# Relu and row sum of 64 MB: the first 8 MB in two contiguous loads, and a piece of the tail moved from ScalarE to VectorE

## The chip, the cores and the metric

The kernel runs on one core of a Trainium2 chip. The metric is device time in microseconds of that core; lower is better. A run on one core has a span (first to last instruction in the profile) about 1.35 us shorter than its time. All runs with several rounds are of the fast state; single runs have no state ("unknown"). Nothing here uses TensorE, so its clock plays no part.

## The reference

```python
def setup_inputs():
    batch, seq, dim = 32, 512, 1024
    return {"x": np.random.randn(batch, seq, dim).astype(np.float32)}

def reference(x):
    relu_x = np.maximum(x, 0)
    return np.sum(relu_x, axis=-1).astype(np.float32)
```

67.1 MB are read, 65 KB written. There are 16384 rows of 4 KB, 128 for each partition.

## The kernel before

All loads go out on SyncE's queue. A buffer holds 16 rows a partition (8 MB); there are three. The first 8 MB are a region of their own, in which partition p owns rows 16p to 16p+15, so 64 KB lie together and the pitch from partition to partition is 64 KB too. The other 56 MB have a pitch of 448 KB.

```python
N1 = P * ROWS                                            # 128 x 16 rows
xf = x_flat[:N1].rearrange("(p m) d -> p m d", p=P)      # first 8 MB
xv = x_flat[N1:].rearrange("(p m) d -> p m d", p=P)      # the rest
# [...]
for j in range(NB):                                      # seven loads of 8 MB
    # [...]
    loaded = load(buf[:, :, :], rows(m, ROWS), j >= NBUF and freed[j - NBUF])
    # [...]
    for n in TWO[j]:                                     # [16], [8, 8] or [7, 7] rows
        clamp(buf[:, c : c + n, :], act_waits)           # ScalarE: relu in place
        total(buf[:, c : c + n, :], m + c, n)            # VectorE: sum of each row
        # [...]
    # [...] single rows of the last two of these loads
```

The last 8 MB come in loads of 8 and 4 rows, then the last four rows in four loads that grow smaller: two rows and the start of the third ("split") row; the end of the split row with the fourth row; and the middle of the split row in two pieces. Partial sums of the split row are written as extra columns behind the last piece, and one VectorE instruction sums that piece and the columns.

```python
act_row(buf[:, c, :], res[:, m : m + 1], loaded)                 # ScalarE: row 0
# [...]
act_row(flat[:, at + split : at + b], others[0], None)           # ScalarE: 340 columns of the split row
piece_act = n_act
dve_row(buf[:, c + 1, :], res[:, m + 1 : m + 2], loaded)         # VectorE: row 1
# [...]
loaded = load(flat[:, at + end : at + 4 * D], src[:, end:])
act_row(buf[:, c + 3, :], res[:, m + 3 : m + 4], loaded)         # ScalarE: row 3
dve_row(flat[:, at + end : at + 3 * D], others[1], loaded)       # VectorE: 240 columns
# [...] loads of the pieces, 220 and 224 columns; two stores
for i in range(len(PIECES) - 1):
    dve_row(parts[i][:, :], others[2 + i], arrived[i])           # VectorE: first piece
nc.vector.wait_ge(sems.act, piece_act)
nc.vector.wait_ge(sems.dve, n_dve)
nc.vector.tensor_scalar(out=last[:, :], ..., accum_out=res[:, NT - 2 : NT - 1]
    ).wait_op(arrived[-1], 16, "sem-ge").then_inc(sems.dve, 1)   # VectorE: last piece + partial sums
# [...]
store(NT - 2, 2, n_act, n_dve)
```

Of the kernel before, what the change touches and what calls it, by code (L numbers as in the profile page):

```python
# [7 lines left out]
P = 128  # L8

ROWS = 16  # L10
NBUF = 3


TWO = [[16], [16], [16], [8, 8], [8, 8], [7, 7], []]
ACT = [0, 0, 0, 0, 0, 2, 9]
DVE = [0, 0, 0, 0, 0, 0, 7]



TAIL = [8, 4]  # L20
ACT_PIECE, END_PIECE = 340, 240
PIECES = [220, 224]

EARLY = 1

# [1 line left out]
def kernel(tc: tile.TileContext, x: bass.AP, out: bass.AP):  # L27
    nc = tc.nc
    sems = Semaphores(tc)

    tc.close()
    tc.compile()
    nc.cur_bb = nc.bb_map[tc.start_bb_name]
    body = nc.cur_bb.bb.instructions
    ends = list(body)
    body.clear()
    n_stores = relu_sum(nc, sems, x, out)
    body.extend(ends)


    nc.cur_bb = nc.bb_map[tc.start_bb_name + "_end"]
    nc.cur_bb.bb.instructions.clear()
    nums = sorted(s.num for s in (*sems.loads, sems.act, sems.dve))
    cleared = range(nums[0], nums[-1] + 1)
    assert len(cleared) == len(nums)
    nc.sync.sem_clear(cleared)
    nc.sync.wait_ge(sems.stored, 16 * n_stores).then_inc(sems.stored, -16 * n_stores)
    open_without_barrier(tc, EARLY)


class Semaphores:
    def __init__(self, tc: tile.TileContext):
        n = len(TWO) + len(TAIL) + 2 + len(PIECES)
        self.loads = [tc.alloc_semaphore(f"load{i}") for i in range(n)]
        self.act = tc.alloc_semaphore("act")
        self.dve = tc.alloc_semaphore("dve")
        self.stored = tc.alloc_semaphore("stored")


def relu_sum(nc, sems: Semaphores, x: bass.AP, out: bass.AP):  # L60
    x_flat = x.flatten_outer_dims()
    N, D = x_flat.shape
    NT = N // P
    NB = len(TWO)
    assert N == P * NT == P * ROWS * (NB + 1)
    assert sum(TAIL) == ROWS - 4 and ACT_PIECE + END_PIECE + sum(PIECES) == D

    bufs = [nc.alloc_sbuf_tensor(f"io{i}", [P, ROWS, D], F32) for i in range(NBUF)]
    res = nc.alloc_sbuf_tensor("res", [P, NT], F32)

    extra = len(PIECES) + 1
    parts = [
        nc.alloc_sbuf_tensor(f"piece{i}", [P, w + extra * (i + 1 == len(PIECES))], F32)
        for i, w in enumerate(PIECES)
    ]


    N1 = P * ROWS
    xf = x_flat[:N1].rearrange("(p m) d -> p m d", p=P)
    xv = x_flat[N1:].rearrange("(p m) d -> p m d", p=P)  # L80
    o_flat = out.rearrange("b s -> (b s)")
    of = o_flat[:N1].rearrange("(p m) -> p m", p=P)
    ov = o_flat[N1:].rearrange("(p m) -> p m", p=P)

    def rows(m, n):
        if m < ROWS:
            return xf[:, m : m + n, :]
        return xv[:, m - ROWS : m - ROWS + n, :]

    def sums(m, n):  # L90
        if m < ROWS:
            return of[:, m : m + n], res[:, m : m + n]
        return ov[:, m - ROWS : m - ROWS + n], res[:, m : m + n]

    n_load = n_act = n_dve = n_store = 0

    def load(dst, src, after=None):
        nonlocal n_load
        dma = nc.sync.dma_start(out=dst, in_=src)  # L99
        if after:  # L100
            dma.wait_op(sems.dve, after[1], "sem-ge")
        dma.then_inc(sems.loads[n_load], 16)
        n_load += 1
        return sems.loads[n_load - 1]

    def store(m, n, act, dve):
        nonlocal n_store
        dst, src = sums(m, n)
        nc.sync.wait_ge(sems.act, act)
        nc.sync.dma_start(out=dst, in_=src).wait_op(sems.dve, dve, "sem-ge").then_inc(  # L110
            sems.stored, 16
        )
        n_store += 1

    def clamp(ap, loaded):
        nonlocal n_act
        i = nc.scalar.activation(out=ap, in_=ap, func=RELU)  # L117
        if loaded is not None:
            i.wait_op(loaded, 16, "sem-ge")
        i.then_inc(sems.act, 1)  # L120
        n_act += 1

    def total(ap, m, n):
        nonlocal n_dve
        nc.vector.tensor_reduce(  # L125
            out=res[:, m : m + n], in_=ap, axis=mybir.AxisListType.X, op=ADD
        ).wait_op(sems.act, n_act, "sem-ge").then_inc(sems.dve, 1)
        n_dve += 1

    def act_row(ap, accum_out, loaded):  # L130
        nonlocal n_act
        i = nc.scalar.activation(out=ap, in_=ap, func=RELU, accum_out=accum_out)  # L132
        if loaded is not None:
            i.wait_op(loaded, 16, "sem-ge")
        i.then_inc(sems.act, 1)
        n_act += 1

    def dve_row(ap, accum_out, loaded):
        nonlocal n_dve
        i = nc.vector.tensor_scalar(  # L140
            out=ap,
            in0=ap,
            scalar1=0.0,
            scalar2=None,
            op0=MAX,
            op1=ADD,
            accum_out=accum_out,
        )
        if loaded is not None:
            i.wait_op(loaded, 16, "sem-ge")  # L150
        i.then_inc(sems.dve, 1)
        n_dve += 1

    freed = []
    m = 0
    for j in range(NB):
        buf = bufs[j % NBUF]
        loaded = load(buf[:, :, :], rows(m, ROWS), j >= NBUF and freed[j - NBUF])
        c = 0
        act_waits = dve_waits = loaded  # L160
        for n in TWO[j]:
            clamp(buf[:, c : c + n, :], act_waits)
            total(buf[:, c : c + n, :], m + c, n)
            act_waits = None
            c += n
        for _ in range(ACT[j]):
            act_row(buf[:, c, :], res[:, m + c : m + c + 1], act_waits)
            act_waits = None
            c += 1
        for _ in range(DVE[j]):  # L170
            dve_row(buf[:, c, :], res[:, m + c : m + c + 1], dve_waits)
            dve_waits = None
            c += 1
        assert c == ROWS
        freed.append((n_act, n_dve))
        m += ROWS


    buf = bufs[NB % NBUF]
    c = 0  # L180
    for n in TAIL:
        loaded = load(
            buf[:, c : c + n, :], rows(m, n), None if c else freed[NB - NBUF]
        )
        for i in range(n):
            if i % 2 == 0 or (n == 8 and i == 7):
                act_row(buf[:, c, :], res[:, m : m + 1], loaded if i == 0 else None)
            else:
                dve_row(buf[:, c, :], res[:, m : m + 1], loaded if i == 1 else None)
            c += 1  # L190
            m += 1

    flat = buf[:, :, :].rearrange("p c d -> p (c d)")
    src = rows(m, 4).rearrange("p c d -> p (c d)")
    at = c * D
    split = 2 * D
    b = split + ACT_PIECE
    end = split + D - END_PIECE
    last, w = parts[-1], PIECES[-1]
    others = [last[:, w + i : w + i + 1] for i in range(extra)]  # L200
    loaded = load(flat[:, at : at + b], src[:, :b])
    act_row(buf[:, c, :], res[:, m : m + 1], loaded)
    sums_act = n_act
    act_row(flat[:, at + split : at + b], others[0], None)
    piece_act = n_act
    dve_row(buf[:, c + 1, :], res[:, m + 1 : m + 2], loaded)
    sums_dve = n_dve
    loaded = load(flat[:, at + end : at + 4 * D], src[:, end:])
    act_row(buf[:, c + 3, :], res[:, m + 3 : m + 4], loaded)
    dve_row(flat[:, at + end : at + 3 * D], others[1], loaded)  # L210
    arrived = []
    for part, n in zip(parts, PIECES):
        arrived.append(load(part[:, :n], src[:, b : b + n]))
        b += n
    assert b == end



    store(0, ROWS, *freed[0])
    store(ROWS, NT - ROWS - 2, sums_act, sums_dve)  # L220

    for i in range(len(PIECES) - 1):
        dve_row(parts[i][:, :], others[2 + i], arrived[i])
    nc.vector.wait_ge(sems.act, piece_act)
    nc.vector.wait_ge(sems.dve, n_dve)  # L225
    nc.vector.tensor_scalar(  # L226
        out=last[:, :],
        in0=last[:, :],
        scalar1=0.0,
        scalar2=None,  # L230
        op0=MAX,
        op1=ADD,
        accum_out=res[:, NT - 2 : NT - 1],
    ).wait_op(arrived[-1], 16, "sem-ge").then_inc(sems.dve, 1)
    n_dve += 1
    store(NT - 2, 2, n_act, n_dve)
    return n_store
# [49 lines left out]
```

## Time and profile before

| | before |
|---|---|
| time, median of the first 3 runs | 161.2 us (161.14 to 161.52) |
| span of the profiled run | 159.7 us |
| VectorE / ScalarE / DMA queue, share of the span | 73% / 66% / 98% |
| first 8 MB landed | 21.84 us |
| last load landed | 157.57 us |
| last load to end of span | 2.17 us |

The landings are read from the records of semaphore increments in the trace: a load has landed when the last of its 16 DMA engines has made its increment. The start of the ScalarE instruction that waits for it, some 0.02 us later, shows the same in the timeline. The end of the chain of waits, with columns start, length, what:

```profile
157.73 0.03 issue
157.76 0.05 DVEq L225
157.81 0.07 issue
157.88 0.40 DVE piece L226 x2
```

Between the accumulator's end at 157.73 us and the last sum stand a semaphore instruction of VectorE's queue and two bits of issue: 0.15 us in which VectorE computes nothing.

### The profile page before, as it was taken

To read this page: it belongs to the slowest core of one execution; us is meant where nothing else is said; L and a number is where in the kernel's file an instruction comes from. 1 tells how busy PE (TensorE), PEld (TensorE's weight loads), DVE (VectorE), ACT (ScalarE), POOL (GpSimd) and SP (SyncE) were. 2 spreads that over 40 slices of the span, in tenths; PEclk is the share of its full clock that TensorE was granted. 3 is DMA by queue.
4 is the path that set the end of the run, shared out by engine and by line. 5 is a ranking of instruction groups with operands and counts; after the bars stand their busy time and mean duration, and the time that the engine had idled before them with its cause. 6 is when DMAs were issued, how large, how long until landed. Compare 5 with 4: busy or idle time off the path is not lost.

```text
span 159.7 us, 120 instructions
## 1 busy us (share of the span) xinstructions
DVE 117.2 (73%) x41; ACT 104.7 (66%) x52; POOL 0.2 (0%) x4
## 2 busy tenths in 40 slices
DVE  0000000009999499994999999999999999999985
ACT  3000059990699708996099941999339992499996
POOL 0000000000000000000000000000000000000000
DMA  7996996996997999979979969969969969898993
GB/s 263 525 525 263 525 525 263 525 492 295 525 460 328 525 394 394 525 345 443 525 328 460 525 279 509 525 263 525 525 263 525 492 295 525 345 443 386 414 417 113
DMA packets 2304, 67.18 MB, mean 421 GB/s; under 512 B 640, under 2 KB 896, under 8 KB 1024
## 3 DMA queue, kind: packets, MB, share of 16 engines
q1 hardware_dynamic: 2304, 67.18, 98.0%
HBM read 67.11 MB, written 0.07 MB: 421 GB/s over the span
## 4 chain that ended last, share of the span: by engine, by line
DMA 44%; DVE 33%; ACT 17%; another core or an unknown queue 3%; SPq 1%; issue 0%; DVEq 0%
DMA io<-in_x_dram 44%; DVE res L125 32%; ACT io L117 17%; SPq L99 1%; DVE io L140 0%; DVE piece L226 0%; DVE piece L140 0%; DVEq L225 0%
## 5 line engine op out<-in xcount | busy, mean ns | idle before, releaser
L125 DVE TENSOR_REDUCE res<-io 128x8 f32<-128x8192 f32 (+2 forms) x9 | 101.1, 11287 | 40.0 <-ACT io L117 40.0
L117 ACT ACTIVATE io<-io 128x8192 f32<-128x8192 f32 (+2 forms) x9 | 81.7, 9110 | 47.7 <-DMA io<-in_x_dram 47.7
L132 ACT ACTIVATE io<-io 128x1024 f32<-128x1024 f32 (+1 forms) x21 | 21.3, 1017 | 5.7 <-DMA io<-in_x_dram 5.7
L140 DVE TENSOR_SCALAR_CACHE_REDUCE io<-io 128x1024 f32<-128x1024 f32 (+1 forms) x14 | 15.5, 1157 | 0.9 <-DMA io<-in_x_dram 0.9
L132 ACT ACTIVATION_READ_ACCUMULATOR io<-io 128x1 f32 x21 | 3.9, 187 | 0.0
L117 ACT ACT_TABLE_LOAD x1 | 1.3, 1283 | 0.1
L140 DVE DVE_READ_ACCUMULATOR io<-io 128x1 f32 x14 | 1.2, 82 | 0.0
L226 DVE TENSOR_SCALAR_CACHE_REDUCE piece<-piece 128x227 f32<-128x227 f32 x1 | 0.4, 390 | 0.2 <-DVE piece L140 0.2
L140 DVE TENSOR_SCALAR_CACHE_REDUCE piece<-piece 128x220 f32<-128x220 f32 x1 | 0.4, 378 | 0.0
L271 POOL MEMSET const-bfloat16-1.0<- 128x1 bf16 x1 | 0.1, 102 | 0.0
L271 POOL MEMSET const-uint8-127<- 128x1 uint8 x1 | 0.1, 102 | 0.0
L271 POOL MEMSET const-float32-0.0<- 128x1 f32 x1 | 0.1, 99 | 0.2 <-issue 0.2
L271 POOL MEMSET const-float32-1.0<- 128x1 f32 x1 | 0.1, 99 | 0.0
L140 DVE DVE_READ_ACCUMULATOR piece<-piece 128x1 f32 x1 | 0.1, 85 | 0.0
L226 DVE DVE_READ_ACCUMULATOR piece<-piece 128x1 f32 x1 | 0.1, 83 | 0.0
## 6 DMA issues: line engine op xcount, KB each, us to landing
io<-in_x_dram SPq DMA_DIRECT2D x1, 4096.0 KB, 21.6
io<-in_x_dram SPq DMA_DIRECT2D x1, 2048.0 KB, 26.1
io<-in_x_dram SPq DMA_DIRECT2D x1, 1194.0 KB, 28.5
io<-in_x_dram SPq DMA_DIRECT2D x1, 632.0 KB, 29.6
io<-in_x_dram SPq DMA_DIRECT2D x7, 26.9
piece<-in_x_dram SPq DMA_DIRECT2D x1, 112.0 KB, 29.2
piece<-in_x_dram SPq DMA_DIRECT2D x1, 110.0 KB, 29.4
out_dram<-res SPq DMA_DIRECT2D x1, 55.0 KB, 1.6
```

Source lines behind the costliest of these rows:

```text
L99: dma = nc.sync.dma_start(out=dst, in_=src)
L117: i = nc.scalar.activation(out=ap, in_=ap, func=RELU)
L125: nc.vector.tensor_reduce(out=res[:, m : m + n], in_=ap, axis=mybir.AxisListType.X, op=ADD).wait_op(sems.act, n_act, "sem-ge").then_inc(se ...
L132: i = nc.scalar.activation(out=ap, in_=ap, func=RELU, accum_out=accum_out)
L140: i = nc.vector.tensor_scalar(out=ap, in0=ap, scalar1=0.0, scalar2=None, op0=MAX, op1=ADD, accum_out=accum_out,)
L226: nc.vector.tensor_scalar(out=last[:, :], in0=last[:, :], scalar1=0.0, scalar2=None, op0=MAX, op1=ADD, accum_out=res[:, NT - 2 : NT - 1],) ...
L271: nc = _bacc.Bacc("TRN2", target_bir_lowering=False, num_devices=1)
```

## The change

Its intent: give the loads at the start a smaller pitch and earlier work, take from ScalarE a piece for which VectorE's last sum had to wait, and let that last instruction wait for VectorE's own accumulator in place of the load. The diff is shortened, and a call of several lines is put on one:

```diff
-TWO = [[16], [16], [16], [8, 8], [8, 8], [7, 7], []]
+HEAD = 8
+TWO = [[8, 8], [16], [16], [8, 8], [8, 8], [7, 7], []]
-ACT_PIECE, END_PIECE = 340, 240
-PIECES = [220, 224]
+START_PIECE, END_PIECE = 280, 260
+PIECES = [240, 244]
 ...
-    xf = x_flat[:N1].rearrange("(p m) d -> p m d", p=P)
+    xf = x_flat[:N1].rearrange("(s p m) d -> p s m d", p=P, m=HEAD)
-    of = o_flat[:N1].rearrange("(p m) -> p m", p=P)
+    of = o_flat[:N1].rearrange("(s p m) -> p s m", p=P, m=HEAD)
 ...
+        if j == 0:
+            heads = [load(buf[:, h : h + HEAD, :], rows(h, HEAD)) for h in range(0, ROWS, HEAD)]
 ...
+                act_waits = heads[i]
 ...
-    act_row(flat[:, at + split : at + b], others[0], None)
-    piece_act = n_act
     dve_row(buf[:, c + 1, :], res[:, m + 1 : m + 2], loaded)
     sums_dve = n_dve
+    dve_row(flat[:, at + split : at + b], others[0], None)
 ...
-    nc.vector.wait_ge(sems.act, piece_act)
-    nc.vector.wait_ge(sems.dve, n_dve)
+    nc.vector.wait_ge(arrived[-1], 16)
     nc.vector.tensor_scalar(out=last[:, :], ...
-    ).wait_op(arrived[-1], 16, "sem-ge").then_inc(sems.dve, 1)
+    ).wait_op(sems.dve, n_dve, "sem-ge").then_inc(sems.dve, 1)
```

More of the change, by code (lines that the diff above doesn't have):

```diff
@@ L52, in __init__ @@
     def __init__(self, tc: tile.TileContext):
-        n = len(TWO) + len(TAIL) + 2 + len(PIECES)
+        n = len(TWO) - 1 + ROWS // HEAD + len(TAIL) + 2 + len(PIECES)
         self.loads = [tc.alloc_semaphore(f"load{i}") for i in range(n)]
@@ L65, in relu_sum @@
     assert N == P * NT == P * ROWS * (NB + 1)
-    assert sum(TAIL) == ROWS - 4 and ACT_PIECE + END_PIECE + sum(PIECES) == D
+    assert sum(TAIL) == ROWS - 4 and START_PIECE + END_PIECE + sum(PIECES) == D
     bufs = [nc.alloc_sbuf_tensor(f"io{i}", [P, ROWS, D], F32) for i in range(NBUF)]
@@ L86, in rows @@
         if m < ROWS:
-            return xf[:, m : m + n, :]
+            assert n == HEAD
+            return xf[:, m // HEAD, :, :]
         return xv[:, m - ROWS : m - ROWS + n, :]
@@ L91, in sums @@
         if m < ROWS:
-            return of[:, m : m + n], res[:, m : m + n]
+            assert m == 0 and n == ROWS
+            return of, res[:, :n].rearrange("p (s m) -> p s m", m=HEAD)
         return ov[:, m - ROWS : m - ROWS + n], res[:, m : m + n]
@@ L157, in relu_sum @@
         buf = bufs[j % NBUF]
-        loaded = load(buf[:, :, :], rows(m, ROWS), j >= NBUF and freed[j - NBUF])
         c = 0
-        act_waits = dve_waits = loaded
-        for n in TWO[j]:
+        if j == 0:
+            heads = [
+                load(buf[:, h : h + HEAD, :], rows(h, HEAD))
+                for h in range(0, ROWS, HEAD)
+            ]
+        else:
+            loaded = load(buf[:, :, :], rows(m, ROWS), j >= NBUF and freed[j - NBUF])
+            act_waits = dve_waits = loaded
+        for i, n in enumerate(TWO[j]):
+            if j == 0:
+                assert n == HEAD
+                act_waits = heads[i]
             clamp(buf[:, c : c + n, :], act_waits)
@@ L196, in relu_sum @@
     split = 2 * D
-    b = split + ACT_PIECE
+    b = split + START_PIECE
     end = split + D - END_PIECE
```

## The prediction

> **What bounds the kernel now.** I read four views in this order: the page's busy shares, DMA queue and chain; the sums by stretch of time; the timeline of the first 130 us; the timeline of the last 5 us. The page first:
>
> ```profile
> DVE 117.2 (73%) x41; ACT 104.7 (66%) x52; POOL 0.2 (0%) x4
> ...
> q1 hardware_dynamic: 2304, 67.18, 98.0%
> HBM read 67.11 MB, written 0.07 MB: 421 GB/s over the span
> ## 4 chain that ended last, share of the span: by engine, by line
> DMA 44%; DVE 33%; ACT 17%; another core or an unknown queue 3%; SPq 1%; issue 0%; DVEq 0%
> ```
>
> VectorE and ScalarE are idle for a quarter and a third of the span; the 16 DMA engines are busy for 98% of it. The chain gives VectorE 33%, but that comes from walking back through "buffer free, so the next load is issued"; whether such an issue matters has to be seen in the timeline. The stretches, with columns window, length, busy time of three engines, clock, share of the 16 DMA engines (a packet is booked where it starts) and GB/s:
>
> ```profile
> 1.00:2.00 1.00, 0.00 (x0) 0.40 (x1) 0.00 (x0) 1.00 3.11 1049
> ...
> 4.00:5.00 1.00, 0.00 (x0) 0.00 (x0) 0.00 (x0) 1.00 2.42 1049
> ...
> 40.00:120.00 80.00, 75.76 (x7) 57.03 (x7) 0.00 (x0) 1.00 1.00 433
> ...
> 156.00:157.00 1.00, 0.65 (x2) 1.00 (x4) 0.00 (x0) 1.00 0.89 292
> 157.00:158.00 1.00, 0.83 (x5) 1.00 (x3) 0.00 (x0) 1.00 0.26 64
> ```
>
> From 40 to 120 us the share is 1.00 at 433 GB/s: nothing is lost there. The first two lines are the one loss at the start. Each window holds exactly one packet of 64 KB per engine (16 x 65536 B in 1 us is the 1049 GB/s), so its share is the mean time of a packet: 3.11 us for the first round, 2.42 us for the second. The first round is 0.69 us longer. The packet records behind it say that the 16 first packets took from 2.69 to 3.44 us, ended 0.54 us apart, and that this distance of 0.54 us stays between the fastest and slowest engine to the end. Now the timeline of the middle:
>
> ```profile
> 21.86 13.86 ACT L117 ACTIVATE io<-io 128x16384 f32<-128x16384 f32 x1 [20.45 <-DMA io<-in_x_dram]
> 35.75 17.22 DVE L125 TENSOR_REDUCE res<-io 128x16 f32<-128x16384 f32 x1 [35.75 <-ACT io L117]
> 41.18 13.86 ACT L117 ACTIVATE io<-io 128x16384 f32<-128x16384 f32 x1 [5.47 <-DMA io<-in_x_dram]
> ...
> 118.58 12.24 ACT L117 ACTIVATE io<-io 128x7168 f32<-128x7168 f32 x2 [5.40 <-DMA io<-in_x_dram]
> ```
>
> ScalarE waits 5.4 us for every 8 MB: 41.18 - 21.86 = 19.32 us between two loads. The first buffer is free when the first reduce ends, 35.75 + 17.22 = 52.97 us, and the fourth load is issued then; the third load keeps the queue full until 60.54 us, 7.6 us later. So no issue in the middle is late. The last 5 us:
>
> ```profile
> 155.42 1.22 DVE L140 TENSOR_SCALAR_CACHE_REDUCE io<-io 128x1024 f32<-128x1024 f32 x1 [0.51 <-DMA io<-in_x_dram]
> ...
> 156.47 0.47 ACT L132 ACTIVATE io<-io 128x340 f32<-128x340 f32 x1
> ...
> 157.01 0.40 DVE L140 TENSOR_SCALAR_CACHE_REDUCE io<-io 128x240 f32<-128x240 f32 x1 [0.36 <-DMA io<-in_x_dram]
> ...
> 157.33 0.38 DVE L140 TENSOR_SCALAR_CACHE_REDUCE piece<-piece 128x220 f32<-128x220 f32 x1
> 157.64 0.09 DVE L140 DVE_READ_ACCUMULATOR piece<-piece 128x1 f32 x1
> 157.88 0.39 DVE L226 TENSOR_SCALAR_CACHE_REDUCE piece<-piece 128x227 f32<-128x227 f32 x1 [0.16 <-DVE piece L140]
> ```
>
> Here VectorE is the last engine. Its second-to-last accumulator is out at 157.73, its last instruction begins at 157.88. The last load is not what it waits for: its issue began at about 128.37 us and took 29.2 us to land, so it was there at 157.57. In the chain a semaphore instruction of 0.05 us stands at 157.76 and 0.07 us of "issue" after it.
>
> **What the Trainium skill says.** "DMA: Bandwidth & Descriptors", section Specifications, puts the ceiling of the fabric at 435 GB/s; the trace agrees (433). The same page, section "Latency and other measured facts", reports that copies slow down at large power-of-two row pitches, from 512 KiB up, and calls aliasing of channels an inference; pitches of 64 or 32 KB are below what it tables, and the 64 KB loads here run at full rate after their first packet. Its section "Rules for kernel authors" says that two transfers to disjoint halves serialize on the same 16 engines, so the second half costs no parallelism and brings none. "DVE: Perf Modes", section "The TRN2 errata", says that each VectorE operation on SBUF has a fixed cost beside its cost per element. The trace agrees: from start to start 1.14 us for 1024 columns and 0.32 us for 240, hence 0.82/784 = 1.046 ns a column and 0.07 us fixed.
>
> **The change part by part.** (1) One load of 8 MB becomes two of 4 MB, each contiguous. The one other load of 4 MB took 147.65 - 137.94 = 9.71 us from landing to landing, the 8 MB before it 137.94 - 118.58 = 19.36. Two halves: 19.42, a cost of +0.06 us on the DMA path.
> (2) The first half can be worked on some 9.7 us earlier: ScalarE and VectorE begin at about 12 and 19 us, and the first buffer is free near 21.9 + 7.0 + 8.7 = 37.6 us in place of 53.0 (7.02 and 8.68 us are the durations of such 8-row instructions in the groups by form). The second load still lands at about 41.2 us, so nothing that follows begins earlier. The slack of 7.6 us at the fourth load becomes 23 us. Worth 0.
> (3) The pitch. What it can touch is the first round of packets alone, 0.69 us over the steady time, of which part must be plain latency: even the quickest first packet, the one that began last, took 0.27 us over 2.42. What could be won is at most the rest, some 0.4 us. The engines begin on partitions four apart, so on addresses that are multiples of 256 KB now and of 128 KB after; both are powers of two, and I give it a third, -0.15 us. This term is chosen, not worked out.
> (4) The tail. ScalarE's 340 columns go (0.47 us, off the path: it then waits for the next load anyway). VectorE gets 280 columns. Sizes before are 2388, 1264, 220, 224 columns, after 2328, 1284, 240, 244; the steady rate (512 B a column over all partitions at 433 GB/s is 1.2 ns) brings the first load 0.07 us forward, the second 0.05, the third 0.02, the last 0. VectorE then: row from 155.35 to 156.50 (1.15); 280 columns to 156.86 (0.29 + 0.07); waits for the second load to 156.96; 260 columns to 157.30; 240 columns to 157.62, accumulator out at 157.71. So the moved piece lies in VectorE's former gap of 0.36 us, just. The sum's wait on its own engine is now the instruction's own and the semaphore instruction before it waits for the load, which has landed at 157.57. It should begin about 0.04 us after 157.71 in place of 0.15: 157.75. 247 columns: 0.33 + 0.08, done at 158.16, against 158.28 before. ScalarE's last row is done near 158.11, so it doesn't take over. The last store, 1.4 us, is unchanged: -0.12 us.
> (5) The store of the first 16 rows has twice the stretches of 32 B; it goes out behind the last load and under the tail's arithmetic: 0.
> Sum: +0.06 - 0.15 - 0.12 = -0.21 us; 161.2 - 0.2 = 161.0 us.
>
> **The rivals.** Rival A, the pitch heals the start: the first round drops to the plain latency and the engines stay together. For it: a spread of 0.54 us that never closes, and the last load lands with its slowest engine. Against it: the pitch stays a power of two. Time: 161.2 - 0.4 + 0.06 - 0.12 = 160.7. Rival B, the start is plain latency and the split tail fails: VectorE is late for the second load, because it has 280 columns more. The margin is 156.96 - 156.86 = 0.10 us. Then the time is 161.2 + 0.06 = 161.3, as the wait's gain is eaten. Rival C, earlier arithmetic lets everything begin earlier by some us, as the chain's 33% of VectorE suggests. Against it speak the full queue and the waits of 5.4 us for every load; it would take 155 us or less, which the 154.8 us of packets alone (64 rounds of 64 KB by 2.418 us) plus start and last store forbid.
>
> **Range and chances.** From rival A with a little more (160.5) to rival B with the scatter of the runs, which span 0.38 us (161.4). Two per cent are 3.2 us; the start's whole loss and the whole tail after the last landing (159.73 - 157.57) together are 2.9 us. So faster by over 2% and slower by over 2% get 0.01 each, same 0.98.
>
> **What would show it.** First landing near 12 us, second near 21.9; ScalarE's wait before the third load still about 5.4 us afterwards; the mean of the first packets, now 32 KB, minus that of steady ones: 0.69 if the pitch does nothing, under 0.4 if rival A holds; the last sum beginning within 0.05 us of the accumulator before it; VectorE waiting about 0.1 us for the second tail load. I am wrong if a load in the middle lands later than 19.4 us after the one before, or if the second half leaves a hole in the DMA at 10 us, which its issue at about 0.45 us should exclude.

## The result, and the profile after

The changed kernel takes 161.1 us (median of 6 runs, 161.01 to 161.36), the kernel before 161.17 us (161.04 to 161.63) in the same rounds and those above. The ratio is 0.999, 95% interval 0.9975 to 1.0006: the same. A ratio here is taken from the fast runs of both kernels in the same rounds, so it is not quite the ratio of the medians quoted.

The page of the changed kernel, its span, busy shares and queue:

```profile
span 159.8 us, 123 instructions
...
DVE 117.8 (74%) x44; ACT 104.4 (65%) x51; POOL 0.2 (0%) x4
...
q1 hardware_dynamic: 2576, 67.18, 98.0%
```

Nothing has moved in the balance of the engines. The start, by stretches (columns as in the prediction: window, length, busy times, clock, DMA share, GB/s):

```profile
1.00:2.00 1.00, 0.00 (x0) 0.40 (x1) 0.00 (x0) 1.00 1.89 524
...
4.00:5.00 1.00, 0.00 (x0) 0.00 (x0) 0.00 (x0) 1.00 1.21 524
```

Each window again holds 16 packets, now of 32 KB (524 GB/s for 1 us). The first take 1.89 us, the steady ones 1.21: an excess of 0.68 us, against 0.69 before. The pitch has not healed the start. In the packet records the first packets end from 2.75 to 3.46 us, 0.72 us apart, where before it was 0.54. The timeline of the first loads:

```profile
12.30 7.03 ACT L122 ACTIVATE io<-io 128x8192 f32<-128x8192 f32 x1 [10.90 <-DMA io<-in_x_dram]
19.36 8.69 DVE L130 TENSOR_REDUCE res<-io 128x8 f32<-128x8192 f32 x1 [19.36 <-ACT io L122]
21.97 7.03 ACT L122 ACTIVATE io<-io 128x8192 f32<-128x8192 f32 x1 [2.65 <-DMA io<-in_x_dram]
...
41.32 13.86 ACT L122 ACTIVATE io<-io 128x16384 f32<-128x16384 f32 x1 [12.32 <-DMA io<-in_x_dram]
```

The engines do begin at 12.3 us, but the 8 MB are complete 0.11 us later than before (21.97 against 21.86), and the next load 0.14 us later (41.32 against 41.18). This delay stays to the end: the last load lands at 157.73 us, 0.16 later than before. The tail:

```profile
155.49 1.22 DVE L145 TENSOR_SCALAR_CACHE_REDUCE io<-io 128x1024 f32<-128x1024 f32 x1 [0.42 <-DMA io<-in_x_dram]
...
156.63 0.44 DVE L145 TENSOR_SCALAR_CACHE_REDUCE io<-io 128x280 f32<-128x280 f32 x1
...
157.09 0.42 DVE L145 TENSOR_SCALAR_CACHE_REDUCE io<-io 128x260 f32<-128x260 f32 x1
...
157.76 0.08 DVE L145 DVE_READ_ACCUMULATOR piece<-piece 128x1 f32 x1
157.88 0.41 DVE L238 TENSOR_SCALAR_CACHE_REDUCE piece<-piece 128x247 f32<-128x247 f32 x1
```

The 280 columns lie in VectorE's old gap, and the last sum begins 0.04 us after the accumulator before it (157.76 + 0.08 = 157.84) where it was 0.15. It begins at 157.88 us all the same, as before, since everything ahead of it came later. So one trace shows a gain in the tail and a loss at the start that cancel. Whether the loss belongs to the change or to chance, one trace can't say.

### The profile page after: what moved, and what is told of

Same layout as the page of the kernel before. It is cut to its first block, busy times and chain, and to the rows that moved or that the text cites. A ratio compares the mean times of both kernels' runs of the same rounds, so it can differ in the third digit from the quotient of the medians.

```text
span 159.8 us, 123 instructions
## 1 busy us (share of the span) xinstructions
DVE 117.8 (74%) x44; ACT 104.4 (65%) x51; POOL 0.2 (0%) x4
## 4 chain that ended last, share of the span: by engine, by line
DMA 43%; DVE 34%; ACT 17%; another core or an unknown queue 3%; SPq 1%; issue 0%
DMA io<-in_x_dram 43%; DVE res L130 32%; ACT io L122 17%; DVE io L145 1%; SPq L104 1%; DVE piece L238 0%; DVE piece L145 0%
## 5 line engine op out<-in xcount | busy, mean ns | idle before, releaser
L137 ACT ACTIVATE io<-io 128x1024 f32<-128x1024 f32 x20 | 20.9, 1043 | 6.0 <-DMA io<-in_x_dram 6.0
L145 DVE TENSOR_SCALAR_CACHE_REDUCE io<-io 128x1024 f32<-128x1024 f32 (+2 forms) x15 | 15.8, 1110 | 0.5 <-DMA io<-in_x_dram 0.4
```

The costliest lines, as they stand in the source:

```text
L137: i = nc.scalar.activation(out=ap, in_=ap, func=RELU, accum_out=accum_out)
L145: i = nc.vector.tensor_scalar(out=ap, in0=ap, scalar1=0.0, scalar2=None, op0=MAX, op1=ADD, accum_out=accum_out,)
```

## The experiments

The kernels of a call share a chip, another one in each call, and the runs of the kernel before. All results were correct.

**First call: repeats, and each half of the change alone.** The repeats have no edit.

> The kernel before once more, for the scatter of its trace. If the start's scatter (when each DMA engine begins, 0.61 us apart before and 0.87 us apart after) is chance, this trace's load landings can move by 0.1 us and more against the first one (second load landed at 41.16, last at 157.57 us), and the last sum still begins about 0.15 us after the accumulator before it. If the start is fixed by the layout, landings repeat within 0.05 us.

> The changed kernel once more. Theory S (two halves and the small pitch make the loads land later by a fixed amount, which eats what the tail saves): last load again 0.1 to 0.2 us later than in the repeat of before (157.73 against 157.57 us), ratio 0.999 to 1.000. Theory C (the late landings were chance): last load lands within 0.05 us of before's and the whole is 0.1 us faster, ratio 0.9993.

The start of the change alone is the changed kernel with the old tail (its sizes, ScalarE's piece and the old waits):

```diff
-START_PIECE, END_PIECE = 280, 260
-PIECES = [240, 244]
+START_PIECE, END_PIECE = 340, 240
+PIECES = [220, 224]
+    act_row(flat[:, at + split : at + b], others[0], None)
+    piece_act = n_act
     dve_row(buf[:, c + 1, :], res[:, m + 1 : m + 2], loaded)
     sums_dve = n_dve
-    dve_row(flat[:, at + split : at + b], others[0], None)
-    nc.vector.wait_ge(arrived[-1], 16)
+    nc.vector.wait_ge(sems.act, piece_act)
+    nc.vector.wait_ge(sems.dve, n_dve)
     ...
-    ).wait_op(sems.dve, n_dve, "sem-ge").then_inc(sems.dve, 1)
+    ).wait_op(arrived[-1], 16, "sem-ge").then_inc(sems.dve, 1)
```

> The new head (two contiguous halves) with the old tail. Theory S: slower than before by 0.1 to 0.15 us (ratio 1.0006 to 1.001). Theory C: within 0.05 us of before (ratio 1.000). Had the pitch healed the start: faster by 0.1 us or more, last load landing at 157.4 us or earlier.

The tail alone is the changed kernel with one load of 16 rows at the start, which is the old layout:

```diff
-HEAD = 8
-TWO = [[8, 8], [16], ...
+HEAD = 16
+TWO = [[16], [16], ...
```

> The old head (one load of 8 MB) with the new tail. Prediction's step: the last sum begins 0.04 us after the accumulator before it in place of 0.15, all else 0: 0.1 us faster than before (ratio 0.9993), last load landing as in before. Rival: VectorE now runs through from the third-to-last load on and is itself late, so nothing is won (ratio 1.000).

| run | median us (runs) | ratio to before, 95% interval | first 8 MB landed | last load landed | from there to the end |
|---|---|---|---|---|---|
| before, first trace | 161.17 (6) | | 21.84 | 157.57 | 2.17 |
| before again | 160.99 (1) | unknown | 21.75 | 157.48 | 2.17 |
| changed, first trace | 161.10 (6) | 0.999 (0.9975 to 1.0006) | 21.95 | 157.73 | 2.03 |
| changed again | 161.25 (6) | 1.0002 (0.9989 to 1.0016) | 22.14 | 157.90 | 2.03 |
| start alone | 161.34 (6) | 1.0007 (0.9994 to 1.002) | 21.97 | 157.72 | 2.21 |
| tail alone | 161.05 (5) | 0.999 (0.9977 to 1.0003) | 21.81 | 157.55 | 2.05 |

Before took 161.11 us (median) in this call. No time differs clearly, for all intervals contain 1; the traces do. The end of the chain of waits, first of the tail alone, then of the start alone:

```profile
157.60 0.10 DVE piece L145
157.70 0.02 issue
157.72 0.42 DVE piece L238 x2
```

```profile
157.91 0.03 issue
157.94 0.05 DVEq L239
157.99 0.07 issue
158.06 0.40 DVE piece L240 x2
```

With the new tail there is 0.02 us between accumulator and last sum (0.04 by the timeline), with the old tail 0.15 us again. The start alone begins its last sum at 158.06 us, later than any other kernel of this call. The loss belongs to the new start (theory S); all three traces with it have the first 8 MB at 21.95 us or later, all three without it at 21.84 or earlier. ScalarE's first start on data after that landing, tail alone and start alone:

```profile
21.83 13.86 ACT L122 ACTIVATE io<-io 128x16384 f32<-128x16384 f32 x1 [20.42 <-DMA io<-in_x_dram]
```

```profile
21.99 7.03 ACT L122 ACTIVATE io<-io 128x8192 f32<-128x8192 f32 x1 [2.66 <-DMA io<-in_x_dram]
```

Its size is less sure than its sign. The same kernel's landings moved between two traces by 0.09 us (before) and by 0.17 to 0.19 us (changed), more than the 0.05 us that I had expected of a fixed start, and the last load of "changed again" landed 0.42 us after that of "before again", where theory S had said 0.1 to 0.2.

**Second call: which part of the new start costs.** It changes two things: two loads in place of one, and the order of rows in HBM. The first edit keeps two loads, but each takes 8 of a partition's 16 rows at the old pitch:

```diff
-    xf = x_flat[:N1].rearrange("(s p m) d -> p s m d", p=P, m=HEAD)
+    xf = x_flat[:N1].rearrange("(p s m) d -> p s m d", p=P, m=HEAD)
-    of = o_flat[:N1].rearrange("(s p m) -> p s m", p=P, m=HEAD)
+    of = o_flat[:N1].rearrange("(p s m) -> p s m", p=P, m=HEAD)
```

> Two loads of 8 rows a partition at the old pitch of 64 KB, with the new tail. Theory Split (two loads, packets of 32 KB, make the landings late): second load lands as in the changed kernel, 21.95 to 22.14 us, last at 157.7 to 157.9. Theory Pitch (the layout in HBM does it): as with the old head, 21.75 to 21.84 and 157.5 to 157.57 us.

The second keeps the two contiguous stretches, but in one load:

```diff
-                load(buf[:, h : h + HEAD, :], rows(h, HEAD))
-                for h in range(0, ROWS, HEAD)
-            ]
+                load(buf[:, :, :].rearrange("p (s m) d -> p s m d", m=HEAD), xf)
+            ] * 2
```

> The two contiguous stretches in one load: each partition takes 32 KB from either, so packets of 32 KB and the small pitch, but one issue and one semaphore. Theory Pitch and a theory Packet (the 32 KB packets alone cost it): lands at 21.95 us or later. Theory Issue (the second issue and its semaphore writes cost it): lands at 21.75 to 21.84 us, last at about 157.55.

Two more amplify the split: 16 loads of one row at the old pitch (the first edit with `HEAD = 1` and `TWO[0] = [1] * 16`), and eight contiguous loads of 1 MB (`HEAD = 2`, `TWO[0] = [2] * 8` in the changed kernel).

> The first 8 MB in 16 loads of one row (4 KB packets) at the old pitch of 64 KB: the split amplified eightfold. If each further load of the first 8 MB costs 0.05 us or more on the DMA path, the 16th lands at 22.5 us or later and the whole is 0.7 us slower (ratio 1.004 or more). If only the first packets matter, the 16th lands within 0.3 us of the changed kernel's second half (21.95 to 22.14 us). The first packets of 4 KB also tell the latency: if the 0.67 us is latency they take about 0.8 us; if it is a cost that grows with bytes at the start, less.

> The first 8 MB in eight contiguous stretches of 1 MB with a pitch of 8 KB. Theory Pitch (smaller pitch is worse or better): the start differs from the 16 loads at 64 KB pitch beyond what the count of loads gives; the prediction's hope that a small pitch heals the start would show engines that end their first packets under 0.3 us apart. Theory Split: eight loads, six more than the changed kernel, land a few tenths of a us later than 21.95 us, and the engines end their first packets 0.5 us or more apart as before.

The kernel before took 161.24 us in this call.

| run | median us (runs) | ratio to before, 95% interval | first 8 MB landed | last load landed |
|---|---|---|---|---|
| halves at the old pitch | 160.94 (4) | 0.9979 (0.9961 to 0.9997) | 21.74 | 157.54 |
| both stretches in one load | 161.00 (4) | 0.9984 (0.9966 to 1.0001) | 21.80 | 157.60 |
| 16 rows at the old pitch | 162.87 (4) | 1.0097 (1.0077 to 1.0117) | 23.18 | 159.24 |
| 8 contiguous stretches | 163.65 (4) | 1.0129 (1.0093 to 1.0166) | 22.32 | 159.88 |

The timeline of the halves at the old pitch, for comparison with that of the changed kernel above:

```profile
12.08 7.03 ACT L122 ACTIVATE io<-io 128x8192 f32<-128x8192 f32 x1 [10.67 <-DMA io<-in_x_dram]
...
21.76 7.03 ACT L122 ACTIVATE io<-io 128x8192 f32<-128x8192 f32 x1 [2.65 <-DMA io<-in_x_dram]
```

Two loads alone cost nothing that shows: this kernel lands 0.2 us ahead of the changed one. The theory Split falls, and so does the theory Issue as a reason for the loss, since this kernel has the second issue and semaphore too. The theory Pitch and the theory Packet, in their plain forms, fall with the one load of both stretches: it has the 32 KB packets and the small pitch, and lands at 21.80 us. What is left is the combination, two loads that are each contiguous.

The row of 16 loads shows that many small loads with small packets do cost, 23.18 us against 21.74, some 0.10 us for each of the 14 more. The edit makes the loads and the packets smaller at once, and no run separates the two. From 8 to 20 us its rate is 413 GB/s, where the large packets have 433; over 8 MB that difference is about 0.9 us (an estimate from these two rates), so most of the 1.44 us is a lower steady rate. It also speaks against a plain latency at the start. I had written 0.8 us for the first packets of 4 KB in that case; the first 16 records took 0.31 us on average, 0.15 over the steady 0.16, and the next 16 were 0.19 over it (by their times some of the first 16 are already the second packet of an engine). So the loss is not one wait of 0.7 us before the first data. Nor is it simply a slow rate over the first kilobytes: the rate, 385 GB/s from 2.5 to 3 us, fell again to 270 GB/s from 3 to 4 us, when, by the order of the packets, the second of these loads was read. Why stays open. The total loss of time, 1.6 us, is more than the 0.7 us expected and more than the 1.4 us that the 16th load explains; some of the rest arises at the 4 MB load near 149 us, which took 10.0 us in place of 9.7. One trace does not say why.

The start of the eight stretches does not heal with a pitch of 8 KB: the engines' increments for the first 8 MB lie 0.58 us apart, and it lands at 22.32 us, a few tenths of a us after 21.95, as theory Split had it. Its packets are of 8 KB, so the pitch is not tested alone. Its total time says nothing of the pitch, for another reason. The timeline of its last instruction, with the wait in brackets:

```profile
160.00 0.41 DVE L238 TENSOR_SCALAR_CACHE_REDUCE piece<-piece 128x247 f32<-128x247 f32 x1 [1.78 <-DMA piece<-in_x_dram]
```

The data of the last load were read by 157.6 us as ever, but its 16 semaphore increments trickled in from 157.56 to 159.88 us, while the first store was being written, which in this layout has 1024 stretches of 8 bytes, stands behind that load in the queue and was read from 156.98 to 157.98 us. That the store delays them is inferred from the order in the queue and the times, no run tests it. The changed kernel's store of 256 stretches of 32 bytes shows nothing of it: the last read ends at 157.27 us and the load has landed at 157.73, 0.46 us later, as with the halves at the old pitch (157.08 and 157.54), whose store is not scattered. So the prediction's zero for this store stands.

**Third call: the three starts on one chip, and a large pitch.** The first three are repeats without an edit.

> The halves at the old pitch with the new tail, again, on one chip with the three others. Theory Layout (contiguous halves in two loads make the slowest DMA engine late, 64 KB pitch does not): second half lands at 21.7 to 21.85 us, the time is 160.9 to 161.05 us, 0.1 to 0.3 us under the changed kernel of the same call and 0.1 to 0.3 us under before. Theory Chance (the first look was a lucky start): second half at 21.9 to 22.1 us, time as the changed kernel's within 0.05 us.

> The two contiguous stretches in one load, again. Its first packets read the same addresses in the same sizes as the changed kernel's. Theory Layout of the pitch alone: lands at 21.95 us or later, as the changed kernel. Theory Layout of the region (what matters is that all engines stay in one stretch of 4 MB for the first load's 9.7 us): 21.8 us, as the first look, and 0.1 to 0.2 us under the changed kernel.

> The changed kernel a third time, as the yardstick of this call. Theory Layout: second half lands at 21.9 to 22.15 us, last load 157.7 to 157.9, engines 0.55 us or more apart, time 161.1 to 161.25. Theory Chance: any value from 21.75 on, time within 0.05 us of the two others.

The fourth gives the whole input one pitch of 512 KB and keeps two loads of 8 rows for the first 8 MB:

```diff
-    xf = x_flat[:N1].rearrange("(s p m) d -> p s m d", p=P, m=HEAD)
-    xv = x_flat[N1:].rearrange("(p m) d -> p m d", p=P)
+    xa = x_flat.rearrange("(p m) d -> p m d", p=P)
+    xv = xa[:, ROWS:, :]
         ...
-            return xf[:, m // HEAD, :, :]
+            return xa[:, m : m + n, :]
```

> All 64 MB at one pitch of 512 KB, the first 8 MB in two loads of 8 rows a partition, new tail. If a larger pitch is better for the start (Theory Layout, extrapolated), the second half lands at 21.75 us or earlier and the engines lie 0.4 us or less apart. If large powers of two hurt, as the Trainium skill tables for copies between HBM tensors, the first packets take longer and the second half lands at 22 us or later, the whole is 0.2 us or more slower than the halves at 64 KB. If the pitch is of no account at all, it lands with the halves at 64 KB within 0.05 us.

The kernel before took 161.16 us in this call. "Apart" is the time from the first to the last engine's increment for the first 8 MB.

| run | median us (5 runs each) | ratio to before, 95% interval | first 8 MB landed | apart | last load landed | to the end |
|---|---|---|---|---|---|---|
| halves at 64 KB again | 160.97 | 0.9993 (0.998 to 1.0005) | 21.75 | 0.29 | 157.63 | 2.00 |
| both stretches in one load again | 160.94 | 0.9989 (0.9976 to 1.0002) | 21.83 | 0.54 | 157.62 | 2.01 |
| changed kernel, third time | 161.15 | 0.9997 (0.9983 to 1.001) | 21.93 | 0.60 | 157.73 | 2.06 |
| halves at 512 KB | 161.53 | 1.003 (1.0017 to 1.0042) | 22.30 | 0.72 | 158.07 | 2.06 |

ScalarE's wait for the second half, in the timelines of the halves at 64 KB, the changed kernel and the halves at 512 KB, one line of each:

```profile
21.77 7.03 ACT L122 ACTIVATE io<-io 128x8192 f32<-128x8192 f32 x1 [2.67 <-DMA io<-in_x_dram]
```

```profile
21.96 7.03 ACT L122 ACTIVATE io<-io 128x8192 f32<-128x8192 f32 x1 [2.66 <-DMA io<-in_x_dram]
```

```profile
22.32 7.03 ACT L122 ACTIVATE io<-io 128x8192 f32<-128x8192 f32 x1 [2.66 <-DMA io<-in_x_dram]
```

These three kernels issue the same loads of the same sizes; only the order of rows in HBM differs. The waits for the second half are equal (2.66 or 2.67 us), so the difference lies wholly in the first half, and in the packet records already in the first packet of each engine: the slowest engine ends it at 3.24, 3.43 and 3.79 us. After that the loads of 8 MB follow each other at one rate, every 19.35 us. The halves at 64 KB then lost nearly half of their lead over the changed kernel at one later load, the 4 MB near 147 us, which took 9.80 us in place of 9.71; in their first trace it took 9.70. So where the rows lie matters at the start, and the later loss is not in the other trace of these halves. The effect is not monotonic in the pitch: of these three starts in two loads, 64 KB is best, 32 KB (contiguous halves) worse by 0.2 us, 512 KB by 0.55 us. My extrapolation "a larger pitch is better" is refuted. The second case of that expectation met its numbers (22.30 us, 0.56 us slower than the halves at 64 KB), but not by a lower rate of copying as the Trainium skill tables it ("DMA: Bandwidth & Descriptors", section "Latency and other measured facts"): the steady rate is unchanged.

The one load of both stretches repeats as well: 21.80 and 21.83 us, between the two. As I read its access pattern, its first packets read the same addresses in the same sizes as those of the changed kernel, yet the slowest ends at 3.29 and 3.33 us, against 3.43 to 3.56 in the four traces with contiguous halves. What differs is what stands behind the first packet in each engine's list, and when the engines begin: on average 0.1 to 0.2 us later. So a theory by first addresses alone does not hold; a late beginning alone does not help, for the first packets of the halves at 512 KB begin as late (on average at 1.39 us, the one load's at 1.36, the changed kernel's at 1.18 to 1.23) and end last. What does matter stays open, as does whether the cause sits in HBM or on the way to it.

**The better version.** The halves at 64 KB and the one load of two stretches, each with the new tail, had lower medians than the kernel before in both their calls (160.94 and 161.00 against 161.24 us, then 160.97 and 160.94 against 161.16), and than the changed kernel in the call that they share with it (161.15). Only the first look at the halves, 0.9979, has an interval that leaves out 1; its repeat gave 0.9993. The traces say where it comes from: the early landing of the old layout and the shorter tail together. The tail alone, with one load at the start, has both as well, and its span, 159.61 us, is as short as theirs (159.56 to 159.63); so splitting the first load adds nothing that shows. By the medians the gain is some 0.2 us, about 0.1%, by the spans of the traces 0.02 to 0.17 us (before: 159.73 and 159.65); it is not clear of noise.

## Why the prediction was right

The time, 161.0 us with a range of 160.5 to 161.4, was met: 161.10, 161.25 and 161.15 us. But it was met as a sum of which one term had the wrong sign: all terms are under 0.3 us and the range is 0.9 us wide, so the number could hardly miss, and meeting it is luck as far as the sum goes. Means over traces: the last load lands at 157.53 us with the old start (three traces) and at 157.77 with contiguous halves (four), +0.24 us. From the last landing to the end it is 2.18 us with the old tail (three) and 2.04 with the new one (tail alone and changed kernel, four), -0.14 us. The sum by traces is +0.1 us, the medians of the first result and of the two repeats differ from those of before by -0.07, +0.14 and -0.01 us. The predicted sum was -0.21.

- **The bound.** Right. The queue is 98% busy in both, loads follow each other every 19.35 us whatever the start, and what the last engine loses on its first packet is, with the exceptions told above, still lost at the end.
- **(1) The split, +0.06 us.** Too large. Halves at the same pitch as one load land at 21.74 and 21.75 us, the one load at 21.75 to 21.84. The estimate was taken from one 4 MB load beside an 8 MB load late in the kernel. The amplified split, 0.10 us a load with 4 KB packets, doesn't carry over to two loads with 32 KB packets.
- **(2) Earlier work, 0.** Right. VectorE begins at 19.36 us and the first buffer is free at about 37.7, but ScalarE still waits 5.50 us for the third load. Rival C, a gain of some us, is refuted.
- **(3) The pitch, -0.15 us.** The step that failed, in sign as well as size: about +0.24 us together with the split, which costs nothing by itself at 64 KB. I called it chosen, not worked out, which was fair: nothing stood behind its sign. The first packets kept their excess (0.65 to 0.69 us in the three traces with the old start, 0.68 to 0.76 us in the four with contiguous halves), and the engines moved further apart. Why two contiguous halves start worse is not shown. Nor is the remaining excess "plain latency", as the 4 KB packets show. Rival A, the healed start, is refuted.
- **(4) The tail, -0.12 us.** Right: -0.14. The last sum begins 0.04 us after its accumulator in the changed kernel, VectorE had 0.09 us left before the second tail load, against the 0.10 predicted, and the moved piece took 0.37 us from start to start, against 0.36. The new tail moves the piece and changes the order of the waits at once, and no run has one without the other. In the profile before, ScalarE's piece was out at 157.04 us, 0.7 us before VectorE's accumulator, so it was not what the last sum waited for: by the chain it is the order of the waits that gives 0.11 us or more. By the code the old split could have had that order too; this was not run. Rival B came near the total by a wrong route: the tail did not fail. (The page that the prediction cites for VectorE's fixed cost has the title "VectorE: DVE Perf Modes".)
- **(5) The scattered store, 0.** Right at 32 bytes; the eight stretches warn that it may not stay so at 8.

## What to carry to other kernels

In a kernel whose DMA queue never runs dry, the start of the first load and the work behind the last one are what is left to win, and both show in the trace: here the landings of one kernel repeated to within 0.01 to 0.2 us, while its total scattered by 0.1 to 0.7 us in a call. Judge such a change by its landings, repeat the trace, and try its parts apart. A net of zero can hide a gain and a loss that are better kept and dropped separately, as the tail and the contiguous halves here. When the last instruction waits for several things, let the queue's separate wait instruction take the one that is there early, and the instruction itself the one that comes last; here that made 0.02 to 0.04 us of 0.15.

## What the Trainium skill lacked or had wrong

- "DMA: Bandwidth & Descriptors", section "Latency and other measured facts", on row pitch: it tables the rate of copies between HBM tensors alone, from 512 KiB up, and has no cost of the start. For loads in stretches of 32 and 64 KB a pitch of 512 KB cost nothing in the steady state (19.35 us for 8 MB, 433 GB/s) and 0.55 us at the start, against halves at 64 KB (22.30 and 21.75 us). Under 512 KiB it has nothing; there 32 KB in contiguous halves cost some 0.2 us at the start.
- The same page gives a first-byte latency, a fixed cost and a steady rate of a transfer, but not the longer first packets of a kernel: 3.11 us for 64 KB against 2.42, 1.89 us for 32 KB against 1.21, 0.31 us (mean of the first 16 records) for 4 KB against 0.16, with the engines 0.3 to 0.75 us apart from then on.
- The same page, section "Rules for kernel authors", advises loads of 1 MiB and more and lacks the price of smaller ones in a full queue from SyncE: loads of 512 KB in packets of 4 KB came every 1.28 us, where 512 KB of a large load in packets of 64 KB take 1.21 (count and size of packets changed together).
- No page has that a store of tiny stretches queued behind a load may hold up that load's completion: with 1024 stretches of 8 bytes the last load's increments took until 159.88 us, 2.3 us after its first (one trace; the cause is inferred).
